# A hybrid encoder step on one core: a PSUM bank each for attention and memory, bias rows for two heads at a time, gates copied by ScalarE, the sample's keys fetched two steps sooner, and the rows of w_out in the order of their use

## The chip, the cores and the metric

The kernel runs on one core of a Trainium2 chip. The metric is the device time of one execution in microseconds (us). Three runs of the kernel before took 2756.32, 2762.39 and 2764.4 us; their median is 2762.39.

## The reference

One layer of an encoder computes one inference step for a prompt (2048 positions) and a sample group (8 requests of 16 positions), model width 1024, all in fp32.

```
h = RMSNorm(x) * g0
z = h @ w_in                  # q,k,v of 8 attention heads (64), q,k,v,o of 4 memory heads (128), 8 gates
A = attention: a chunk of 64 sees itself and 8 chunks before it, with a learned bias clipped at +-256
    (sample: 512 cached keys and its own 16)
B = matrix memory: decayed sum of k v^T with exp input gate, log-sigmoid forget gate, running maximum;
    h = num / max(|den|, exp(-m)), then RMSNorm by head, times g and sigmoid(o)
x = x + RMSNorm(concat(RMSNorm(A), B) @ w_out) * g1
x = x + RMSNorm(ConvFFN(RMSNorm(x) * g2)) * g3      # up-projection, causal conv of 3, GELU gate, down
```

Outputs are x of both groups, the last keys and values, the memory state and the conv halo.

## The kernel before

The program is written in a layer that allocates tiles from pools and lets a scheduler order the instructions. The scheduler takes them by their place in the source and moves them where its own model of time says that an engine would be free; each engine then runs its list strictly in order and waits on semaphores. So an edit of a few lines moves instructions on every engine.

The work of the first phase is a projection and, between its matmuls, two pipes of small units. The projection runs over 28 groups: two halves of the tiles (tile = 128 positions; tiles 0 to 7 and the sample, then 8 to 15) times 14 column groups of w_in (`va`, `qk` for attention, `qb`, `vo` for memory). Every product is three matmuls (L105, L106, L107): high times high, high times low, low times high part of fp32 numbers. A group accumulates in one of two PSUM banks `mm`. ScalarE empties it into a staging tile `st` (two of them, L237, L239) and stores that from its own DMA queue (L252, L288), and a 264-column group also holds the gates, which VectorE copied at L286.

The first pipe is attention (`att_stream`). `load_head` (L340 on) fetches a head's bias `nb`, queries and keys by SP's queue and splits them into high and low parts on ScalarE and VectorE. `att_unit` makes scores `s` in a two-bank PSUM tile `big`, adds the bias and takes the row minimum on VectorE, the exponent on ScalarE, transposes (`pt`), splits (`pth`, `ptl`) and multiplies by the values into `ot`; after two heads `ao` transposes the result, which goes to DRAM (`mixd`). The eight heads' bias comes from `relrow`: for every head a row `ext` of 767 numbers is written 128 times to DRAM (L317, 393 KB, SP's queue), two corners of 64x64 are overwritten by a large number (L322, POOL's queue, out of SBUF), and the result is read back along its diagonals. All eight heads are made so at the start. The sample's attention (`attention_sample`) runs over eight batches in two parts: keys (`sk`), scores `ss`, weights, values (`sv`, tail `svt`), result `sot`; keys and values use two buffers each of the tags `kh` and `kl`.

The second pipe is the memory (`mem_stream`): `prep_prompt` and `prep_sample` make cumulated gates, and `mlstm` runs over chunks of 128 positions for four heads. A chunk has two steps. The first computes scores and transposed keys in a PSUM tile `ms` (L701 on), the exponent `w` and the scaled keys `kw`; the second computes three products in a PSUM tile `ma` (L715 to L717) and updates the state `cst`. In the kernel before, a new chunk's first step may be issued ahead of the old one's second.

PSUM has eight banks: two for `mm`, two double ones for `big`, and two under the tag `sm`, which attention's `ot`, `ao`, `sot`, the memory's tiles and later the FFN's transposes take in turn.

`pump` steps the two pipes in turn so that the work of VectorE keeps a share of that of TensorE. At the last group `w_out_steps` casts the rows of w_out into high and low parts `wo` (L946 on), 128 rows at a time, two column halves each. Then `project` multiplies the 17 tiles by w_out, 48 matmuls a tile (24 for each half of the columns), with the transposes `mT_pt` of the next tile between the halves; in tiles 0 to 7 and the sample, `mT_pt` uses the two banks `mm`. Beside it, `folds` turns w_down into sums that the FFN uses, by DMAs of POOL's queue and subtractions on VectorE. When tile 8 is loaded, the two pipes are emptied (`drain`), the first phase's memory is released (`open_ffn`), and units that normalise and transpose finished tiles for the FFN (`h2_units`, `h2T_pt`, rows `x2r`) take the pipes' place. The FFN follows and fills the second half of the time; the change does not touch it, apart from where its transposes find their banks.

Of the kernel before, what the change touches and what calls it, by code (L numbers as in the profile page):

```python
# [50 lines left out]
def hymba_step(ctx: ExitStack, tc: tile.TileContext, I: dict, O: dict):  # L51
# [14 lines left out]

    def ps_sm(name):
        return psum.tile([P, 512], F32, tag="sm", name=name)
# [72 lines left out]
    pm = p1.enter_context(tc.tile_pool(name="pm", bufs=2))  # L141

# [128 lines left out]
    def group_rows(wh, wl, half, chunks, dst, name, width=256, out=None):  # L271
        for ci, tiles in enumerate(HALVES[half]):
            for j, t in enumerate(tiles):
                ch = chunks[ci]
                acc = ps_mm(f"{name}_{t}")
                for k in range(KT):
                    w = slice(k * width, (k + 1) * width)
                    tt = slice(j * P, (j + 1) * P)
                    mm3(acc[:, :width], ch[:, 0, k, tt], ch[:, 1, k, tt], wh[:, w], wl[:, w],
                        start=(k == 0), stop=(k == KT - 1))  # L280
                    if k % 4 == 3:
                        yield 1.3, 0.0
                stage = pa.tile([P, 384], F32, tag="st", name=f"{name}_st{t}", bufs=2)
                evac_scaled(stage[:, :256], acc[:, :256], None)
                if width > 256:
                    nc.vector.tensor_copy(gates[:, gate_ix(t), :], acc[:, 256:width])  # L286
# [6 lines left out]
    relrow = dt_([HA, P, SQ], "relrow")  # L293
# [9 lines left out]

    def build_bias():
        ext = dt_([HA, SQ], "ext")

        def unit():
# [8 lines left out]
            for h in range(HA):  # L316
                tc.keep_in_program_order(nc.sync.dma_start(relrow[h], ext[h:h + 1, :].broadcast_to([P, SQ])))  # L317
                yield 0.0, 0.0
                for r, c in ((0, 576), (64, 0)):
                    at = bias_src(h, P, 640)  # L320
                    at = bass.AP(at.tensor, at.offset + r * (SQ - 1) + c, [[SQ - 1, 64], [1, 64]])
                    nc.gpsimd.dma_start(at, big[r:r + 64])  # L322
                if h % 2:
                    yield 0.0, 0.0
# [56 lines left out]
    def att_unit(s, g2, j):  # L381
# [45 lines left out]
        ot = ps_sm(f"ot{h}_{i0}")  # L427
# [21 lines left out]
        ao = ps_sm(f"ao{pair}_{kg}")  # L449
# [94 lines left out]
    def cum_rows(ig, lf, nlf, r, trim, name):  # L544
        ba = ps_sm(f"ba{name}")
# [9 lines left out]
    def pack_columns(pk, name):  # L555
        pt = ps_sm(f"pkT{name}")
# [7 lines left out]
    def prep_prompt(half):  # L564
# [8 lines left out]
        rt = ps_sm(f"rt{half}")  # L573
# [9 lines left out]
        mp = ps_sm(f"mp{half}")  # L583
# [90 lines left out]
    def mlstm(h, half):  # L674
# [22 lines left out]
        def chunk(s, c):  # L697
# [4 lines left out]
            sp = ps_sm(f"ms{s.nm}_{c}")  # L702
# [12 lines left out]
            nc.tensor.matmul(acc[:, e:2 * e], q_, cst[h], start=True, stop=True)  # L715
            nc.tensor.matmul(acc[:, 0:e], w, s.va[:, c, :], start=True, stop=True)
            nc.tensor.matmul(acc[:, 2 * e:3 * e], kw, s.va[:, c, :], start=True, stop=True)  # L717
            nc.vector.scalar_tensor_tensor(cst[h], cst[h], dec[:, cc, h:h + 1], acc[:, 2 * e:3 * e],
                                           op0=ALU.mult, op1=ALU.add)
            nc.scalar.activation(num[:, c, :], acc[:, e:2 * e], AF.Identity, scale=col(1))  # L720
            nc.vector.tensor_tensor(num[:, c, :], num[:, c, :], acc[:, 0:e], op=ALU.add)
# [15 lines left out]
        for s in pairs:  # L737
            if s.pc < 3:
                yield load(pairs[s.pc + 1])
            yield chunk(s, 0)  # L740
            yield chunk(s, 1)

    def mlstm_sample(h):
# [6 lines left out]
        def own():  # L750
# [16 lines left out]
            sp = ps_sm(f"ms{nm}")  # L767
# [8 lines left out]
            acc = ps_sm(f"ma{nm}")  # L776
# [5 lines left out]
        def batches(bp):  # L782
# [13 lines left out]
            cu = ps_sm(f"cu{nm}_{bp}")  # L796
# [39 lines left out]
    def attention_sample(b0, b1):  # L836
# [18 lines left out]
        def scores(b):  # L855
            ks = halves(f"sk{b}")
# [3 lines left out]
            if b % 4 == 0 or b == b0:  # L860
                nc.sync.dma_start(own, kTs[:, :, b // 4 * 64:b // 4 * 64 + 64])
            yield 0.0, 0.0
# [34 lines left out]
        def values(b):  # L897
# [6 lines left out]
            yield 0.0, 0.0  # L904
            yield 0.0, 0.0
            yield 0.0, 0.0
            yield 0.0, 0.0
            ot = ps_sm(f"sot{b}")
# [28 lines left out]
    def w_out_steps():  # L937
# [5 lines left out]
        for k in range(KT):  # L943
# [9 lines left out]
            h_, l_ = big[-1][:, k % 3 * 2, :], big[-1][:, k % 3 * 2 + 1, :]  # L953
            for c in (slice(0, 512), slice(512, D)):
# [4 lines left out]
                else:  # L959
                    nc.scalar.copy(h_[:, c], raw[:, c])  # L960
                    nc.vector.tensor_tensor(l_[:, c], raw[:, c], h_[:, c], op=ALU.subtract)
                if k < 6:
                    yield 0.0, 0.6
            wo.append((h_, l_))
# [88 lines left out]
    def open_ffn():  # L1053

        p1.close()
        ffn.p3 = ctx.enter_context(tc.tile_pool(name="p3", bufs=2, reuse_waits="tile"))
# [939 lines left out]
```

## Time and profile before

| | |
|---|---|
| runs | 2756.32, 2762.39, 2764.4 us, median 2762.39 |
| profiled execution | 2761.56 us, span 2759.8 us |
| busy | PE 2659.9 us (96%), VectorE 1862.4 (67%), ScalarE 1417.6 (51%), POOL 700.7 (25%) |
| mean granted clock of TensorE | 0.988 |
| stages, from the page and the timeline | projection with attention and memory to about 1010 us, w_out to about 1330, FFN from there |

A line of a stretch gives the time, for each engine its busy time and in brackets its number of instructions, the granted clock, the share of DMA time and GB/s. A line of waits gives the waiting instruction, who released it, the total, the count and the longest. In a line of the timeline the first two numbers are start and duration, and square brackets hold the idle time of the engine before it and what ended that. PE is TensorE, DVE is VectorE, ACT is ScalarE.

### The profile page before, as it was taken

What the parts mean: (1) busy time and instruction counts of PE and PEld (TensorE: products, weight loads), DVE (VectorE), ACT (ScalarE), POOL (GpSimd) and SP (SyncE); (2) the same over time, 40 slices, a digit from 0 to 9 for tenths busy, and PEclk for the clock granted to TensorE, in tenths of its full rate; (3) what the DMA queues carried; (4) which work ended last, traced back from release to release, by engine and by line L of the source; (5) the groups of instructions that cost most, each with busy time, mean ns of one, the idle gap of its engine ahead of it and who ended that gap; (6) DMA issues with size and microseconds to landing.
All of it is one profiled execution on the core that took longest, in us unless ns stands there. A gap on an engine that the chain in (4) does not pass through costs nothing.

```text
span 2759.8 us, 47655 instructions
## 1 busy us (share of the span) xinstructions
PE 2659.9 (96%) x16459; PEld 2481.2 (90%) x16459; DVE 1862.4 (67%) x3536; ACT 1417.6 (51%) x2887; POOL 700.7 (25%) x1325
## 2 busy tenths in 40 slices
PE   8899999999999999979899999999999999999998
PEld 7899999999799998867799998889999878999976
DVE  5345445644355666556898998758888776899956
ACT  4345544533355665433454456655454665555554
POOL 1100000211000002344655542023333212466401
PEclk9999999999999999989999999999999999999999
DMA  5634454556743554469877768766786777788775
GB/s 173 171 114 138 122 186 140 172 176 196 225 135 116 157 178 146 146 228 308 298 246 215 214 198 265 251 208 195 223 219 192 228 252 238 213 246 237 253 257 183
DMA packets 333711, 555.70 MB, mean 201 GB/s; under 512 B 61762, under 2 KB 169374, under 8 KB 333150
## 3 DMA queue, kind: packets, MB, share of 16 engines
q1 hardware_dynamic: 250798, 405.03, 47.5%
q0 software_dynamic: 44080, 113.81, 14.1%
q10 hardware_dynamic: 38592, 33.83, 3.7%
q8 instruction: 129, 2.11, 0.3%
q14 instruction: 112, 0.92, 0.1%
HBM read 389.77 MB, written 172.18 MB: 204 GB/s over the span
## 4 chain that ended last, share of the span: by engine, by line
PE 41%; DMA 5%; DVE 4%; issue 2%; ACT 1%; POOL 0%; DVEq 0%; SPq 0%; POOLq 0%; ACTq 0%
PE uec L105 5%; PE uec L106 5%; PE uec L107 5%; PE dn L107 3%; PE dn L105 3%; PE dn L106 3%; PE ua L107 3%; PE ua L106 3%; PE ua L105 3%; DMA wu<-in_w_up 2%; PE dnm L107 1%; PE dnm L106 1%; PE dnm L105 1%; PE ub L107 1%; PE ub L106 1%
## 5 line engine op out<-in xcount | busy, mean ns | idle before, releaser
L105 PE MATMUL uec<-B,wuh 128*128 128x384 f32 (+1 forms) x720 | 236.6, 329 | 9.2 <-DVE ug L1495 5.9
L106 PE MATMUL uec<-B,wuh 128*128 128x384 f32 (+1 forms) x720 | 235.4, 327 | 0.0
L107 PE MATMUL uec<-B,wul 128*128 128x384 f32 (+1 forms) x720 | 234.3, 327 | 0.0
L1324 ACT CAST wuh<-wu 128x512 fp32r<-128x512 f32 x255 | 141.6, 618 | 102.6 <-PE uec L106 98.7
L107 PE MATMUL dn<-wdh,al 128*128 128x512 f32 x462 | 186.0, 403 | 3.4 <-DVE al L1325 3.4
L105 PE MATMUL dn<-wdh,ah 128*128 128x512 f32 x462 | 183.6, 397 | 5.9 <-ACT ah L1324 4.0
L1325 DVE TENSOR_TENSOR al<-ar,ah 128x768 fp32r<-128x768 f32 (+2 forms) x141 | 108.4, 779 | 118.4 <-ACT ah L1324 114.8
L106 PE MATMUL dn<-wdl,ah 128*128 128x512 f32 x462 | 182.8, 396 | 0.0
L1324 ACT CAST ah<-ar 128x768 fp32r<-128x768 f32 (+2 forms) x141 | 96.2, 692 | 153.2 <-PE dnm L106 113.9
L1325 DVE TENSOR_TENSOR wul<-wu,wuh 128x512 fp32r<-128x512 f32 x255 | 164.3, 682 | 2.4 <-ACT wuh L1324 2.4
L663 POOL TENSOR_SCALAR ad<-ad 128x2 f32<-128x2 f32 x32 | 6.3, 195 | 615.3 <-DVE ad L661 615.3
L410 DVE CUSTOM_DVE_ANT_0 tmp<-s,nb 128x640 f32<-128x640 f32 (+4 forms) x128 | 94.1, 737 | 100.1 <-PE s L400 99.5
L105 PE MATMUL vo<-wi_h,hT 128*128 128x256 f32 x544 | 155.5, 286 | 0.0
L107 PE MATMUL vo<-wi_h,hT 128*128 128x256 f32 x544 | 155.3, 285 | 0.0
L106 PE MATMUL vo<-wi_l,hT 128*128 128x256 f32 x544 | 154.9, 285 | 0.0
L1325 DVE TENSOR_TENSOR wdl<-wdr,wdh 128x512 fp32r<-128x512 f32 x231 | 145.3, 684 | 8.2 <-ACT wdh L1324 8.0
L105 PEld LDWEIGHTS uec<-B,wuh 128*128 128x128 f32 x720 | 135.2, 188 | 13.6 <-issue 6.8
L105 PE MATMUL qk<-hT,wi_h 128*128 128x384 f32 (+1 forms) x384 | 130.3, 339 | 9.9 <-ACT qk_st L239 6.2
L411 ACT ACTIVATE tmp<-tmp,mn 128x640 f32<-128x640 f32 (+4 forms) x128 | 97.7, 763 | 77.0 <-DVE mn L410 72.6
L106 PEld LDWEIGHTS uec<-B,wuh 128*128 128x128 f32 x720 | 135.4, 188 | 0.2
L107 PEld LDWEIGHTS uec<-B,wul 128*128 128x128 f32 x720 | 135.1, 188 | 0.0
L1324 ACT CAST wdh<-wdr 128x512 fp32r<-128x512 f32 x231 | 127.4, 619 | 11.8 <-PE uec L106 7.4
(473 smaller groups left out, 9101.8 us busy)
## 6 DMA issues: line engine op xcount, KB each, us to landing
wu<-in_w_up SPq DMA_DIRECT2D x220, 256.0 KB, 4.8
wu<-wsd SPq DMA_DIRECT2D x176, 256.0 KB, 4.7
wdr<-wtd SPq DMA_DIRECT2D x132, 256.0 KB, 5.1
wi_raw<-in_w_in SPq DMA_DIRECT2D x52, 512.0 KB, 4.2
wdr<-in_w_down SPq DMA_DIRECT2D x99, 256.0 KB, 4.7
wsd<-ws POOLq DMA_DIRECT2D x88, 256.0 KB, 4.8
ar<-ad_S SPq DMA_DIRECT2D x50, 384.0 KB, 4.0
kraw<-kTd SPq DMA_DIRECT2D x112, 128.0 KB, 3.1
```

Source lines behind the costliest of these rows:

```text
L105: nc.tensor.matmul(out, ah, bh, start=start, stop=False, skip_group_check=onto)
L106: nc.tensor.matmul(out, ah, bl, start=False, stop=False, skip_group_check=onto)
L107: nc.tensor.matmul(out, al, bh, start=False, stop=stop, skip_group_check=onto)
L410: nc.vector.tensor_tensor_reduce(o_, s_, b_, 1.0, 3e38, ALU.add, ALU.min, accum_out=mn)
L411: nc.scalar.activation(tmp[:, :n], tmp[:, :n], AF.Exp, bias=mn, scale=-1.0, accum_out=rsum[:, i % 4, hh:hh + 1])
L663: nc.gpsimd.tensor_scalar(ad, ad, 1.0 / DH, 0.0, op0=ALU.mult, op1=ALU.add)
L1324: nc.scalar.copy(h, r)
L1325: nc.vector.tensor_tensor(l, r, h, op=ALU.subtract)
```

## The change

Five edits. (1) In the first phase attention's `ot`, `ao` and `sot` use one PSUM bank of their own (`at`) and the memory's tiles another (`me`); the two banks `sm` exist only from the FFN on. A memory chunk now uses one tile: its three products overwrite scores and keys in the same bank, and the stream has an empty step (`bubble`) after each chunk, or the next load. (2) Bias rows of heads 0 and 1 are made at the start; those of head h + 2 when head h's second group of keys is loaded. The corners come from a copy in DRAM. (3) The gates are copied by ScalarE. (4) The sample's keys of the next batch are fetched in the second step of the values of this one. (5) For rows 6 and 7 of w_out the first column half of both is cast before the second.

The diff, cut to its core:

```diff
+    def ps_at(name):
+        return sm.pool.tile([P, 512], F32, tag="at", name=name, bufs=1)
+
+    def ps_me(name):
+        return sm.pool.tile([P, 512], F32, tag="me", name=name, bufs=1)
+
     def ps_sm(name):
-        return psum.tile([P, 512], F32, tag="sm", name=name)
+        return sm.pool.tile([P, 512], F32, tag="sm", name=name, bufs=2)
...
-                    nc.vector.tensor_copy(gates[:, gate_ix(t), :], acc[:, 256:width])
+                    nc.scalar.copy(gates[:, gate_ix(t), :], acc[:, 256:width])
...
+    def bias_rows(h):
+        tc.keep_in_program_order(nc.sync.dma_start(relrow[h], ext[h:h + 1, :].broadcast_to([P, SQ])))
+        for r, c in ((0, 576), (64, 0)):
+            at = bias_src(h, P, 640)
+            at = bass.AP(at.tensor, at.offset + r * (SQ - 1) + c, [[SQ - 1, 64], [1, 64]])
+            nc.gpsimd.dma_start(at, corner[r:r + 64])
...
-            for h in range(HA):
...
+            nc.sync.dma_start(corner, big)
+            for h in range(2):
+                bias_rows(h)
...
     def load_head(s):
         pair, kg, hh, h, nm = s.pair, s.kg, s.hh, s.h, s.nm
+        if kg == 1 and h < HA - 2:
+            bias_rows(h + 2)
...
-            sp = ps_sm(f"ms{s.nm}_{c}")
+            sp = ps_me(f"ms{s.nm}_{c}")
...
-            acc = ps_sm(f"ma{s.nm}_{c}")
-            nc.tensor.matmul(acc[:, e:2 * e], q_, cst[h], start=True, stop=True)
...
+            own, upd, old = sp[:, 0:e], sp[:, e:2 * e], sp[:, 2 * e:3 * e]
+            nc.tensor.matmul(old, q_, cst[h], start=True, stop=True)
...
         for s in pairs:
-            if s.pc < 3:
-                yield load(pairs[s.pc + 1])
             yield chunk(s, 0)
+            yield load(pairs[s.pc + 1]) if s.pc < 3 else bubble()
             yield chunk(s, 1)
+            yield bubble()
...
             nc.sync.dma_start(tail, vs[b * DS:(b + 1) * DS, :])
             yield 0.0, 0.0
+            if b + 1 < b1:
+                fetch(b + 1)
...
             for c in (slice(0, 512), slice(512, D)):
                 if k < 6:
+                    cast(k, raw, c)
                     yield 0.0, 0.6
+                elif k == 7:
+                    cast(6, late[:, :D], c)
+                    cast(7, late[:, D:], c)
```

What the scheduler makes of it, at three places. First POOL at the start, where it computes the scales of the first tiles (`n_4_ms`, `n_4_rs`: tile 4's mean square and its inverse root). Before:

```order
L94 TENSOR_TENSOR n_3_rs<-n_3_ms,nhalf 128x1
L88 TENSOR_SCALAR n_4_ms<-ssq_501 128x1
L94 TENSOR_TENSOR n_4_rs<-n_4_ms,nhalf 128x1
L88 TENSOR_SCALAR n_5_ms<-ssq_552 128x1
L94 TENSOR_TENSOR n_5_rs<-n_5_ms,nhalf 128x1
```

And now, with the corners of heads 0 and 1 (`relrow_301`, `relrow_302`):

```order
L100 TENSOR_TENSOR n_3_rs<-n_3_ms,nhalf 128x1
L318 DMA relrow_301<-corner 64x64
L94 TENSOR_SCALAR n_4_ms<-ssq_513 128x1
L318 DMA relrow_301<-corner 64x64
L318 DMA relrow_302<-corner 64x64 x2
L100 TENSOR_TENSOR n_4_rs<-n_4_ms,nhalf 128x1
```

The four corner writes, which stood behind the scales of all tiles, have moved between the two instructions of tile 4's.

Second SP's queue from the first bias rows to the first keys of the second group, in the new order (`nb` is a head's bias, `xr` a tile's x, `wi_raw` weights, `relrow_303` and `relrow_304` the rows of heads 2 and 3):

```order
L314 DMA relrow_301<-ext 128x767
L314 DMA relrow_302<-ext 128x767
L1256 DMA wi_raw_404<-in_w_in 128x1024
L232 DMA xr_562<-in_x_prompt 128x1024
L1256 DMA wi_raw_509<-in_w_in 128x1024
L356 DMA nb_0_1165<-relrow_301 128x640
L356 DMA nb_0_1229<-relrow_302 128x640
L232 DMA xr_663<-in_x_prompt 128x1024
...
L314 DMA relrow_303<-ext 128x767
L363 DMA qraw_1_1389<-qTd_1_98 64x512 x2
L366 DMA kraw_1_0_1390<-kTd_0_81 64x512 x2
```

The bias of the first two heads is read ahead of tile 7's x (`xr_663`); before, the bias rows stood behind all loads of x (the first four between two loads of weights, `wi_raw_945` and `wi_raw_1161`), and the reads of the bias behind them.

Third TensorE in the projection by w_out, around a memory chunk (`ms`, `ma`) and the transposes of the next tile (`mT_pt`). Before:

```order
L77 MATMUL mT_pt_14352<-ident,mr_14269 128x128 x4
L715 MATMUL ma_10_1_13118<-cst_313,mqk_10_12793 128x129
L716 MATMUL ma_10_1_13118<-mvo_10_12795,w_10_1_13074 128x129
L717 MATMUL ma_10_1_13118<-mvo_10_12795,kw_10_1_13076 128x129
L77 MATMUL pt_12_13152<-ident,tmp_12_13092 128x128 x5
L399 MATMUL s_14_13238<-kh_3_12827,qs_3_12829 128x320
L400 MATMUL s_14_13238<-kl_3_12828,qs_3_12829 128x320
```

And now, at one of the closest handovers of the memory's bank:

```order
L727 MATMUL ms_14_1_13495<-cst_325,mqk_14_13380 128x129
L728 MATMUL ms_14_1_13495<-mvo_14_13382,w_14_1_13498 128x129
L729 MATMUL ms_14_1_13495<-mvo_14_13382,kw_14_1_13500 128x129
L83 MATMUL mT_pt_14007<-ident,mr_13835 128x128 x4
L83 MATMUL mT_pt_14014<-ident,mr_13835 128x128 x4
L715 MATMUL ms_8_0_13716<-mqk_8_13672 128x128
L83 MATMUL ms_8_0_13716<-ident,mqk_8_13672 128x128
L111 MATMUL wo_1_14032<-wo_13346,mt_13758 128x512
```

Before, attention's matmuls (`pt`, `s`) still stood between those of the projection here; now they have all gone before, and only memory chunks are left. In the new order attention's last matmul stands behind 120 of the projection's 816 (before: 353), the memory's last behind 431 (before: 517), and 92 stand between the memory's last and the FFN's first transposes `h2T_pt` (before: 59).

More of the change, by code (lines that the diff above doesn't have):

```diff
@@ L290, in group_rows @@
                     nc.scalar.dma_start(out[s - 3][:, 0 if s == 4 else t % 4, :], stage[:, :256])
-    relrow = dt_([HA, P, SQ], "relrow")
+    relrow = [dt_([P, SQ], f"relrow{h}") for h in range(HA)]
+    ext = dt_([HA, SQ], "ext")
+    corner = dt_([P, 64], "corner")
     def raw_tile(name):
@@ L713, in chunk @@
             num = s.num
-            acc = ps_sm(f"ma{s.nm}_{c}")
[L715 to L721, printed above, removed]
+            own, upd, old = sp[:, 0:e], sp[:, e:2 * e], sp[:, 2 * e:3 * e]
+            nc.tensor.matmul(old, q_, cst[h], start=True, stop=True)
+            nc.tensor.matmul(own, w, s.va[:, c, :], start=True, stop=True)
+            nc.tensor.matmul(upd, kw, s.va[:, c, :], start=True, stop=True)
+            nc.vector.scalar_tensor_tensor(cst[h], cst[h], dec[:, cc, h:h + 1], upd, op0=ALU.mult, op1=ALU.add)
+            nc.scalar.activation(num[:, c, :], old, AF.Identity, scale=col(1))
+            nc.vector.tensor_tensor(num[:, c, :], num[:, c, :], own, op=ALU.add)
             yield 0.65, 0.47
@@ L853, in halves, with fetch @@
             return [pa.tile([P, 1024], F32, tag=tag, name=f"{name}{tag}", bufs=2) for tag in ("kh", "kl")]
-        def scores(b):
-            ks = halves(f"sk{b}")
+        keys = {}
+        def fetch(b):
+            keys[b] = ks = halves(f"sk{b}")
             for i in range(2):
@@ L861, in scores @@
                 nc.sync.dma_start(own, kTs[:, :, b // 4 * 64:b // 4 * 64 + 64])
+        def scores(b):
+            if b not in keys:
+                fetch(b)
+            ks = keys.pop(b)
             yield 0.0, 0.0
@@ L907, in values @@
             yield 0.0, 0.0
[L908 removed]
+            ot = ps_at(f"sot{b}")
             for kk in range(5):
```

38 lines of the change are left out of this document (17 added, 21 removed).

## The prediction

> **What bounds the kernel now.** I read the page first, then the stretches, then the waits of PE, then the stretches around those waits.
>
> ```profile
> span 2759.8 us, 47655 instructions
> PE 2659.9 (96%) x16459; PEld 2481.2 (90%) x16459; DVE 1862.4 (67%) x3536; ACT 1417.6 (51%) x2887; POOL 700.7 (25%) x1325
> ```
>
> TensorE is busy 2659.9 of 2759.8 us, and the change keeps every matmul: it can win only from what TensorE loses, 99.9 us of idle time and the slow time behind it. Next, stretches (columns: us, busy of PE, PEld, DVE, ACT, POOL with instructions, granted clock, DMA share, GB/s): the start, the tail of attention and memory under the w_out matmuls, and the way into the FFN.
>
> ```profile
> core 0: us, PE busy (x) PEld busy (x) DVE busy (x) ACT busy (x) POOL busy (x), PEclk, DMA share, GB/s
> 12.00:45.00 33.00, 32.46 (x248) 31.98 (x248) 22.49 (x30) 19.51 (x34) 6.23 (x14) 1.00 0.53 168
> 1000.00:1180.00 180.00, 173.02 (x1030) 150.73 (x1028) 114.17 (x262) 99.56 (x260) 41.94 (x87) 0.98 0.54 168
> 1180.00:1330.00 150.00, 125.83 (x559) 99.91 (x558) 87.81 (x142) 51.61 (x116) 71.73 (x134) 0.91 0.81 272
> ```
>
> The last row loses 24.2 us and a clock of 0.91; nothing in it is saturated (DVE 59%, DMA 0.81), so these are chains of latency. PE's waits, those that the argument uses (us in total, times, longest):
>
> ```profile
> PE h2T_pt L1111 <- DVE x2r L1103: 7.7, 3, 6.0
> PE qk L105 <- ACT qk_st L239: 6.2, 1, 6.2
> PE ss L874 <- DMA sk6kh<-in_cache_k: 3.2, 1, 3.2
> PE qk L105 <- ACT qk_st L237: 3.1, 1, 3.1
> PE va L105 <- DVE gates L286: 2.3, 1, 2.3
> PE mT_pt L77 <- DVE mr L995: 2.3, 2, 2.1
> PE ms L703 <- DVE w L709: 1.9, 1, 1.9
> PE wo L106 <- DVE wo L961: 1.4, 1, 1.4
> PE ma L715 <- DVE attT L442: 1.1, 1, 1.1
> ```
>
> A wait costs more than its length. Stretches around them, PE alone, with two of dense work (57 to 64 only 384-column matmuls, 1206 to 1216 only w_out):
>
> ```profile
> 57.00:64.00 7.00, 7.00 (x42) 1.00 0.77 226
> 77.00:90.20 13.20, 8.91 (x36) 0.74 0.75 146
> 104.40:114.00 9.60, 3.41 (x11) 0.64 0.96 284
> 150.00:400.00 250.00, 250.00 (x1835) 1.00 0.46 140
> 534.00:541.00 7.00, 4.68 (x26) 0.76 0.56 174
> 709.00:718.20 9.20, 5.92 (x30) 0.81 0.90 320
> 1012.00:1036.00 24.00, 19.78 (x121) 0.86 0.76 229
> 1140.00:1200.00 60.00, 54.45 (x283) 0.97 0.59 188
> 1206.00:1216.00 10.00, 10.00 (x45) 1.00 0.79 248
> 1217.00:1241.00 24.00, 14.00 (x51) 0.64 0.77 267
> ```
>
> A projection matmul issues every 7.00/42 = 0.167 us, one of w_out every 10/45 = 0.222. So 77 to 90.2 needed 36 x 0.167 = 6.0 us and took 13.2 (7.2 lost), 104.4 to 114 lost 9.6 - 11 x 0.167 = 7.8, and 1217 to 1241 at least 24 - 51 x 0.222 = 12.7.
>
> **The bias rows.** Both early waits (9.3 us, 15.0 lost) lie beside the eight writes of bias rows and their sixteen corners.
>
> ```profile
> L317 SPq DMA_DIRECT2D relrow<-ext x8: 469/576/2191, 58.8 to 101.6; - x8
> ...
> DMA to landing us min/median/max: 7.1/8.2/9.5
> ...
> 109.57 0.62 ACT L363 CAST kh<-kraw 128x512 fp32r<-128x512 f32 x1 [4.29 <-DMA kraw<-kTd]
> 110.10 0.48 ACT L239 ACTIVATE qk_st<-qk 128x384 f32<-128x384 f32 x1
> ```
>
> ScalarE waited 4.29 us in its order for keys (issued behind the last two row writes) and only then emptied the bank that TensorE wanted. With two heads first and six spread over the next pairs, queues are shorter. But after the change the rows of heads 2 and 3 still stand before key loads on SP's queue. A full win is 15.0, none 0; I take 9.0, the middle and a little, since one write at a time replaces two to six. Spreading adds six writes of 7.1 to 9.5 us beside stores that double-buffered stages wait for; between 150 and 400 us PE was never idle, so they have cover: 1.0 (0 to 4).
>
> **What they cost at the start.** The first two heads' corners now stand in POOL's queue between the scales of tiles 3 and 4, and the loads of their bias stand in SP's queue ahead of tile 7's x. In the trace:
>
> ```profile
> L322 POOL DMA_DIRECT2D relrow<-outside x16: 532/532/759, 66.2 to 110.4; - x16
> ...
> DMA to landing us min/median/max: 2.8/7.0/8.1
> ...
> 12.55 0.29 SPq L312 DMA_DIRECT2D ext<-relf  x1
> 19.99 0.19 POOL L88 TENSOR_SCALAR n_ms<-ssq 128x1 f32<-128x1 f32 x1 [5.09 <-ACT hT L229]
> 25.20 0.65 SPq L225 DMA_DIRECT2D xr<-in_x_prompt  x1
> 37.84 0.33 SPq L225 DMA_DIRECT2D xr<-in_x_sample  x1
> ```
>
> A row write can go out at about 16 us (behind ext's landing), lands 7 us later, and so POOL gets to tile 4's scale near 24 to 26 instead of 20. In the new order 47 more matmuls of tiles 2 and 3 (0.13 us each by 33/248) stand ahead of tile 4's transposes, 6 us: that covers it. Tile 7's x waits for a corner's landing (7.0 in the median), so it goes out at 30 to 32 instead of 25.2; the sample's x, whose place tile 7 frees, follows at 40 or later instead of 37.84. Cost 3.0 (0 to 8).
>
> **Gates by ScalarE.**
>
> ```profile
> L286 DVE COPY gates<-va x17: 153/157/167, 23.2 to 560.0; 128x8 f32<-128x8 f32 x17
> ```
>
> Seventeen copies of 0.157 us leave DVE; in its order they stood behind splits and held a bank. 534 to 541 needed 26 x 0.13 = 3.4 us and took 7.0: 3.6 gone. ScalarE, which has just emptied the same bank, is 51% busy; with no cover, and at twice the time each, the copies would cost 17 x 0.314 = 5.3, and I take nothing.
>
> **The clock.** The stretch at 534 shows a granted clock of 0.76 after a wait of 2.3 us. The Trainium skill, "TensorE: Matmul & The Clock Gate", What's actually happening, says that the clock halves after an idle window of about 3.4 us and comes back after as long a busy one. This trace halves it after shorter waits; by the page the gates would bring 2.3, not 3.6.
>
> **Keys two steps sooner.** 3.2 us of wait, and half a clock for 3.4 us behind it (0.81 over 9.2 us is 1.7): 4.9. The load is moved behind the values' loads of the batch before, whose waits for buffers it now shares on SP. In the new order the eight batches stand evenly, with 72 projection matmuls or so from one to the next (12 us at 0.167 for 2 MB, 175 GB/s, below the 320 of the stretch at 709). I take 4.5 (0 to 5).
>
> **A bank each.** The wait of ma for attT (1.1) goes. But memory now reuses one bank for scores, update and next scores, 98 tiles in all, and attention one for 88. Between two of them TensorE mostly has other work: of 184 handovers 5 have under 2 us, counting what stands between them in the order at the trace's rates. Five times that 1.1 us would be 5.5; I take 1.5 (0 to 5.5).
>
> **Rows of w_out.** The first half of tile 0 no longer waits for the second half's columns: 1.4 and its clock. 1012 to 1036 lost 4.2 of idle and 24 x 0.14 = 3.4 of clock over three waits; I take 3.0 (1.4 to 7.6).
>
> **The moved tail.** The extra steps of memory and the free bank move work: attention now ends 120 w_out matmuls into the projection instead of 353, memory at 431 instead of 517 of 816. That is both cost and gain. Cost: (353 - 120)/48 = 4.9 tiles more without attention between them. 1140 to 1200, where attention had ended, is idle for 5.55 us and 1.8 of clock in 60 us, 4.5 tiles; so 4.9 tiles would cost 8.0, and the memory chunks that remain there cover some: 6.0 (0 to 28). Gain: the FFN's first transposes need the space of the phase that ends.
>
> ```profile
> 1204.05 0.35 DVE L718 SCALAR_TENSOR_TENSOR cst<-cst,dec,ma 128x129 f32<-128x129 f32 x1 [1.67 <-PE ma L717]
> 1209.34 0.13 DVE L1058 MEMSET halo<- 128x88 f32 x1
> 1223.05 1.28 DVE L1103 SCALAR_TENSOR_TENSOR x2r<-x2r,n_rs,g 128x1024 f32<-128x1024 f32 x1 [0.74 <-POOL n_rs L94]
> ```
>
> From the last chunk to the scaled row passed 20.3 us. TensorE had 59 w_out matmuls for it (13.1 us) and waited 6.0 at the half clock that follows. Now 92 stand there (20.4 us): the wait goes, with most of the 12.7 lost. I take 9.0 (4 to 12.7).
>
> **Sum.** -9.0 + 1.0 + 3.0 - 3.6 - 4.5 - 1.1 + 1.5 - 3.0 + 6.0 - 9.0 = -18.7 us. The profiled execution took 2761.6 (1.8 outside its span), 0.8 under the median of 2762.4; 2761.6 - 18.7 = 2743. With the page's clock rule for the gates the sum would be -17.4.
>
> **Rivals.** First, the rows don't really move: with the writes still beside the keys, both early waits stay and the start is paid in full (8.0): -18.7 + 9.0 + 5.0 = -4.7, 2757. For it: ScalarE's order still has the cast of the keys ahead of a bank to empty. Against: less is in flight, and the store of the first wait (L237) has no row write left before it. Second, idle time only moves into the projection: if the 4.9 uncovered tiles pay what the tile at 1180 to 1189 pays, its waits for mr (2.1) and for w (1.9) and the clock behind them (1.8 by the row of that stretch), 5.8 each, they cost 28 instead of 6: +3, 2765. For it: the banks of mT_pt are those of w_out there. Third, slower: the single banks. A matmul into the one bank must wait until ScalarE and VectorE have read it. If one handover in four waits 1.1 us, 46 x 1.1 = 51 instead of 1.5: 2792; it decides from (18.7 + 8.3)/1.1 = 25 waits on. The Trainium skill, "Perfetto Trace Analysis", Matmuls, has independent groups rotate through different banks so that emptying one overlaps the next; by that rule this rival is due. Against it: the trace holds one such wait (1.1, of ma for attT), and the new order keeps the handovers apart.
>
> **Chances.** The forecast 0.62 (on its own 2725 to 2757: two or three terms at their bounds, not all), the first rival 0.13, half of it a small gain, the second 0.16, slower 0.09. A difference under 0.3% (8.3 us) can't be told from none. Faster: 0.62 + 0.08 = 0.70; within 0.3%: 0.05 + 0.16 = 0.21; slower 0.09. The range leaves out the third rival and the ends of the others: 2722 to 2765.
>
> **What would show it.** Right: no wait of qk for qk_st over 2 us before 130 us; none of va for gates; none of ss for a key; the first h2T_pt under 2 us; clock 0.95 or more from 1180 to 1330. PE's loss from 12 to 50 us up by some 3 us. Wrong: a row of waits of ms or ot for num, cst or attT (single banks), or of mT_pt for mx and mr that sum to over 20 us (moved idle time), or 15 us lost in the first 50 us.

## The result

Four runs of the changed kernel took 2728.1 to 2736.4 us, median 2731.5; the kernel before 2756.3 to 2764.4 (four runs, one more than above), median 2761.0. The ratio is 0.9899, with a 95% interval of 0.9878 to 0.9920: 28 us faster by the ratio (the medians lie 29.5 apart). A second series, of the same code built and loaded once more, took 2737.2 to 2744.2 (six runs), median 2741.1, beside 2758.6 for the kernel before (17 runs): 0.9934, interval 0.9918 to 0.9949, 18 us faster; it had been expected at 2728 to 2736. The two series don't overlap; what that means for the experiments stands at their head. The forecast was 2743, between 2722 and 2765, a gain of 18.7. One run of the experiment e3 below took 3696 us at a mean granted clock of 0.654 and is left out of e3's median.

A correction to what stands above: the counts of w_out matmuls behind which attention and memory end (353 and 120, 517 and 431) are each one tile, 48, too high. In the traces attention's last stands behind 305 of them before and 72 after, memory's last behind 469 and 383, and the FFN's first transposes behind 528 and 475. The differences, with which the forecast worked (59 and 92 matmuls of cover, 4.9 tiles), are the same.

### The profile page after: what moved, and what is told of

Read it like the earlier page. It is cut to its first block, busy times and chain, and to the rows that moved or that the text cites. A ratio compares the mean times of both kernels' runs of the same rounds, so it can differ in the third digit from the quotient of the medians.

```text
span 2734.6 us, 47676 instructions
## 1 busy us (share of the span) xinstructions
PE 2652.1 (97%) x16459; PEld 2476.5 (91%) x16459; DVE 1862.9 (68%) x3519; ACT 1418.7 (52%) x2904; POOL 685.8 (25%) x1325
## 4 chain that ended last, share of the span: by engine, by line
PE 45%; DVE 3%; DMA 3%; issue 1%; ACT 1%; POOL 0%; DVEq 0%; POOLq 0%; SPq 0%; ACTq 0%
PE uec L111 6%; PE uec L112 6%; PE uec L113 6%; PE dn L113 4%; PE dn L111 4%; PE dn L112 4%; PE ua L113 3%; PE ua L112 3%; PE ua L111 3%; PE dnm L113 2%; PE ub L113 1%; PE dnm L112 1%; PE ub L111 1%; PE ub L112 1%; PE dnm L111 1%
## 5 line engine op out<-in xcount | busy, mean ns | idle before, releaser
L435 DVE TENSOR_TENSOR ptl<-pt,pth 128x640 fp32r<-128x640 f32 (+4 forms) x128 | 93.6, 737 | 58.6 <-ACT pth L434 57.7
```

The source lines that it names most:

```text
L435: nc.vector.tensor_tensor(s.ptl[:, sl, qc], ptv, s.pth[:, sl, qc], op=ALU.subtract)
```

## The profile after

The head of the page of the changed kernel:

```profile
span 2734.6 us, 47676 instructions
...
PE 2652.1 (97%) x16459; PEld 2476.5 (91%) x16459; DVE 1862.9 (68%) x3519; ACT 1418.7 (52%) x2904; POOL 685.8 (25%) x1325
```

TensorE's idle time has gone from 99.9 to 82.5 us. For what the slower clock costs beside it, a stretch is read so: its width less busy time times granted clock is what TensorE lost there, idle and slow together. First the kernel before, stretch by stretch (us, PE, PEld, DVE, ACT, POOL, clock, DMA share, GB/s):

```profile
12.00:75.00 63.00, 59.59 (x413) 57.60 (x414) 36.09 (x89) 26.54 (x50) 10.78 (x23) 1.00 0.54 161
75.00:130.00 55.00, 44.52 (x254) 42.95 (x254) 14.87 (x38) 17.34 (x40) 5.41 (x12) 0.88 0.58 155
...
600.00:700.00 100.00, 99.09 (x786) 91.39 (x785) 43.67 (x153) 35.62 (x105) 14.04 (x49) 1.00 0.65 199
700.00:775.00 75.00, 67.56 (x587) 58.73 (x586) 27.38 (x59) 30.81 (x69) 1.26 (x4) 0.98 0.67 207
1000.00:1050.00 50.00, 45.70 (x297) 41.35 (x296) 35.40 (x79) 32.73 (x81) 8.94 (x19) 0.93 0.73 216
1050.00:1215.00 165.00, 158.37 (x879) 134.67 (x879) 97.23 (x230) 77.28 (x211) 44.80 (x91) 0.99 0.49 154
1215.00:1330.00 115.00, 94.78 (x412) 74.62 (x411) 69.36 (x95) 41.15 (x85) 59.94 (x111) 0.90 0.89 302
1330.00:1600.00 270.00, 258.78 (x1443) 252.27 (x1442) 250.16 (x386) 131.50 (x207) 150.21 (x213) 0.99 0.73 235
```

And the changed kernel:

```profile
12.00:75.00 63.00, 56.27 (x374) 53.88 (x375) 33.93 (x68) 26.68 (x57) 10.22 (x19) 0.95 0.46 150
75.00:130.00 55.00, 49.70 (x288) 47.30 (x286) 19.30 (x60) 20.40 (x52) 3.32 (x7) 0.94 0.60 150
...
600.00:700.00 100.00, 94.29 (x891) 83.36 (x890) 38.71 (x125) 36.71 (x104) 9.97 (x33) 1.00 0.81 249
700.00:775.00 75.00, 72.37 (x511) 70.73 (x510) 43.85 (x116) 38.08 (x90) 6.88 (x22) 1.00 0.45 134
1000.00:1050.00 50.00, 48.45 (x405) 48.05 (x404) 32.23 (x73) 32.92 (x76) 2.17 (x6) 1.00 0.50 153
1050.00:1215.00 165.00, 153.05 (x759) 123.83 (x758) 89.25 (x188) 62.45 (x171) 61.52 (x122) 0.97 0.63 201
1215.00:1330.00 115.00, 107.10 (x524) 88.51 (x523) 81.26 (x110) 48.49 (x96) 53.60 (x96) 1.00 0.90 317
1330.00:1600.00 270.00, 265.33 (x1504) 262.51 (x1503) 253.32 (x397) 134.98 (x216) 139.53 (x220) 0.99 0.71 220
```

From 1215 to 1330 us the kernel before lost 115 - 94.78 x 0.90 = 29.7 us, and the changed one 115 - 107.10 x 1.00 = 7.9. That is 21.8 of the 25.2 us by which the spans differ. The other stretches shown add up to 7 us less, out of terms of both signs: the start loses 9.5 instead of 3.4, the stretch with the two early waits 8.3 instead of 15.8, the sample's keys 2.6 instead of 8.8 while 600 to 700 just ahead of them loses 5.7 instead of 0.9, 1000 to 1050 loses 1.5 instead of 7.5, w_out with memory beside it 16.5 instead of 8.2, and the FFN's entrance 7.3 instead of 13.8. Of those not shown, 400 to 600 loses 1.6 instead of 6.3 and 775 to 1000 4.8 instead of 0.6. From 12 to 2700 us all this comes to 28 us, not 25.2: the clock is printed to two places, which leaves a loss open by up to half a us for every 100 us, and a fixed stretch doesn't hold quite the same work in both kernels.

PE's waits that answer to the forecast's list:

```profile
PE cus L809 <- DMA cs<-in_state_c: 3.1, 2, 2.2
PE va L111 <- ACT gates L293: 2.9, 2, 1.5
PE ms L727 <- DVE w L721: 2.8, 4, 1.4
...
PE ms L715 <- DVE num L732: 1.5, 2, 1.1
...
PE h2T_pt L1139 <- DVE x2r L1131: 0.5, 1, 0.5
```

No qk waits for qk_st, no ss for a key and no ma for attT; h2T_pt's 7.7 us are 0.5. The waits for gates have not gone, they only have another engine's name: 2.3 on VectorE before, at 536 us; now 1.4 at 28 us and 1.5 at 555 on ScalarE. New is the wait of the sample's memory for its state, cs (3.1, in the stretch from 600 to 700). The 2.8 for w are waits for the product's input, and of the waits of ms only the 1.5 for num are for the single bank.

## The experiments

Medians of twelve kernels, each timed in five rounds beside the kernel before, and what TensorE lost in the stretches above (worked out in the same way from the stretches of each one's trace). "Ends" gives the w_out matmuls behind which attention's last, memory's last and the FFN's first transposes stand.

| kernel | us | ratio (95%) | ends | 12-75 | 75-130 | 700-775 | 1000-1050 | 1050-1215 | 1215-1330 | 1330-1600 |
|---|---|---|---|---|---|---|---|---|---|---|
| before | 2755 to 2761 | 1 | 305, 469, 528 | 3.4 | 15.8 | 8.8 | 7.5 | 8.2 | 29.7 | 13.8 |
| changed | 2731.5 | 0.9899 (0.9878-0.9920) | 72, 383, 475 | 9.5 | 8.3 | 2.6 | 1.5 | 16.5 | 7.9 | 7.3 |
| e12 changed, again | 2741.1 | 0.9934 (0.9918-0.9949) | 72, 383, 475 | 9.9 | 7.6 | 1.7 | 1.9 | 19.2 | 8.5 | 9.5 |
| e1 bias rows only | 2745.4 | 0.9948 (0.9929-0.9966) | 208, 352, 480 | 8.8 | 5.0 | 4.4 | 6.5 | 18.1 | 10.4 | 8.5 |
| e2 edit 1 only | 2738.2 | 0.9929 (0.9915-0.9942) | 72, 383, 475 | 3.0 | 11.6 | 2.1 | 0.2 | 16.6 | 7.7 | 5.9 |
| e3 edits 3, 4, 5 only | 2755.4 | 0.9990 (0.9975-1.0006) | 305, 469, 528 | 3.9 | 16.6 | 8.3 | 8.0 | 7.4 | 28.7 | 10.2 |
| e4 empty steps only | 2739.6 | 0.9931 (0.9916-0.9945) | 120, 332, 471 | 2.8 | 15.0 | 10.7 | 1.2 | 22.5 | 7.1 | 4.4 |
| e5 banks, no steps | 2737.0 | 0.9927 (0.9904-0.9950) | 72, 336, 480 | 3.5 | 13.4 | 2.3 | 1.6 | 12.7 | 7.5 | 5.8 |
| e6 cover only | 2753.0 | 0.9987 (0.9972-1.0002) | 305, 469, 568 | 3.8 | 15.6 | 8.0 | 10.4 | 6.1 | 30.8 | 11.9 |
| e7 whole without banks | 2736.3 | 0.9935 (0.9912-0.9959) | 120, 332, 480 | 5.7 | 5.3 | 4.7 | 0.6 | 18.6 | 7.5 | 3.4 |
| e8 rows behind x | 2731.9 | 0.9909 (0.9886-0.9931) | 72, 383, 475 | 4.0 | 8.6 | 3.0 | 2.1 | 17.9 | 8.5 | 9.5 |
| e9 whole, less cover | 2750.3 | 0.9970 (0.9958-0.9981) | 72, 383, 432 | 9.9 | 8.5 | 0.8 | 2.1 | 25.8 | 4.0 | 13.8 |
| e10 whole without 3, 4, 5 | 2736.3 | 0.9914 (0.9898-0.9931) | 72, 383, 475 | 8.0 | 6.5 | 2.2 | 2.2 | 18.4 | 11.7 | 5.4 |
| e11 banks, rows, no steps | 2744.1 | 0.9944 (0.9928-0.9959) | 72, 336, 480 | 4.0 | 11.1 | 3.0 | 0.8 | 13.8 | 14.6 | 9.8 |

The medians of the kernel before lie between 2755.4 and 2761.0 in its four series. Those of the changed kernel lie 9.5 us apart, and its runs within a series spread by 7 to 8. Three chips were used, one for e1 to e4, one for e5 to e8 and one for e9 to e12; the record doesn't name that of the first series, so the 9.5 us may come from the chip as well as from the loading. So a kernel is read against the kernel before, and a difference of under some 10 us between two kernels counts here only where a wait or a stretch of the traces shows it as well.

### The bias rows alone (e1)

```diff
-            for h in range(HA):
...
+            for h in range(2):
+                bias_rows(h)
...
+        if kg == 1 and h < HA - 2:
+            bias_rows(h + 2)
```

> The kernel before with edit 2 alone (bias rows two heads at a time). In the new order attention ends after 208 w_out matmuls instead of 305, memory after 352 instead of 469, and 128 matmuls stand ahead of the FFN's first transposes instead of 59, although no line there is touched. Theory A (the forecast's: a term belongs to the place of its edit; the tail belongs to edit 1): only the start changes, by 75 to 130 us some 6.6 less lost and from 12 to 75 us some 6.2 more, as the trace of the whole change shows: 2758 to 2763. Theory B (the tail is a matter of the order that comes out, whichever edit brings it; 128 matmuls are 28 us of cover for a chain of 20): the first wait of h2T_pt for x2r is under 1 us, the stretch 1200 to 1350 loses some 16 us less, and the total is 2738 to 2748.

Measured 2745.4, 14 us faster by the ratio of 0.9948. Two of its stretches:

```profile
75.00:130.00 55.00, 51.54 (x319) 49.27 (x318) 19.75 (x55) 22.71 (x58) 3.29 (x7) 0.97 0.60 157
...
1215.00:1330.00 115.00, 107.81 (x508) 87.52 (x507) 79.81 (x108) 47.74 (x95) 60.61 (x108) 0.97 0.91 318
```

At its own place it gains what was forecast and pays for it: 75 to 130 loses 5.0 instead of 15.8, 12 to 75 loses 8.8 instead of 3.4. But 1215 to 1330 loses 10.4 instead of 29.7, though not a line of that stage is edited, and the first wait of h2T_pt is gone (four later ones for x2r sum to 3.7). Theory B holds, theory A falls. (The old unit for the bias took thirteen steps of attention's pipe, the new one three. That this is what moves attention up is argued from the code, not shown.)

### Edit 1 alone (e2), and its two halves (e4, e5)

Edit 1 is the separate banks, the chunk's products in the scores' bank, and the empty steps. e4 is only the latter:

```diff
         for s in pairs:
-            if s.pc < 3:
-                yield load(pairs[s.pc + 1])
             yield chunk(s, 0)
+            yield load(pairs[s.pc + 1]) if s.pc < 3 else bubble()
             yield chunk(s, 1)
+            yield bubble()
```

> The kernel before with edit 1 alone (a bank each, products of memory in one tile, empty steps). The order ends attention after 72 w_out matmuls, memory after 383, and has 92 ahead of the first FFN transposes, as the whole change has. Theory A (the tail belongs to edit 1): the first h2T_pt wait goes (16 us) and so do the waits of mt and ug between 1250 and 1600 us (13 together); -20 to -29 with the early waits of qk for qk_st and the gates' wait still there: 2732 to 2742. Rival (the tail's gain needs another edit as well, the banks cost): the h2T_pt wait stays over 2 us or waits of ms for num and cst sum to over 5 us: 2750 or more.

> The kernel before with only the empty steps of the memory's stream (and its loads one step later), banks as before. Attention ends after 120 w_out matmuls, memory after 332, 139 ahead of the first FFN transposes. If the tail is a matter of the order (theory B): h2T_pt's first wait is gone and the total is 2735 to 2748, the banks themselves being worth nothing or a little less than nothing. If the separate banks are what frees the tail (theory A): the h2T_pt wait or its like stays, 2755 or more.

> The kernel before with the separate banks alone: one bank for attention, one for memory, the products of a chunk in the scores' bank, and none of the empty steps, so a new chunk's scores may be issued right behind the old one's products. The order ends attention after 72 w_out matmuls, memory after 336, and has 144 ahead of the first FFN transposes. If the forecast's third rival holds (46 handovers at 1.1 us), the waits of ms, ot and pt for num, cst, attT and mx grow by some 50 us: 2775 or more. If only the order counts: the first h2T_pt wait is gone as with the empty steps alone, 2738 to 2746.

Measured: 2738.2, 2739.6 and 2737.0 (1 us under the range expected for e5), ratios 0.9929, 0.9931 and 0.9927. Either half gives what both give, and each alone about as much as the whole change in its second series. e4's tail:

```profile
1050.00:1215.00 165.00, 150.02 (x760) 123.38 (x759) 89.59 (x209) 64.42 (x183) 56.75 (x116) 0.95 0.60 194
1215.00:1330.00 115.00, 107.86 (x523) 87.80 (x522) 80.33 (x107) 50.36 (x97) 62.48 (x104) 1.00 0.92 316
```

And in e5, with single banks and no empty step between the chunks, the only waits of ms for the bank's reader (num is added out of it), with its tail:

```profile
PE ms L710 <- DVE num L727: 1.6, 3, 0.6
```

```profile
1215.00:1330.00 115.00, 107.54 (x528) 89.52 (x527) 81.25 (x111) 46.98 (x91) 54.65 (x97) 1.00 0.91 315
```

1.6 us in three waits, where the third rival wanted 51: single banks cost next to nothing here, even without the steps that keep the chunks apart. (The same wait is 3.2 in e2 and 3.3 in e11; with shared banks it is 1.5 in e1 and 1.4 in e7.) And what the changed kernel gains in the tail isn't the banks' own either, since the empty steps, with the banks as before, gain it too.

### The three local edits alone (e3), and the whole without them (e10)

```diff
-                    nc.vector.tensor_copy(gates[:, gate_ix(t), :], acc[:, 256:width])
+                    nc.scalar.copy(gates[:, gate_ix(t), :], acc[:, 256:width])
...
+            if b + 1 < b1:
+                fetch(b + 1)
...
+                elif k == 7:
+                    cast(6, late[:, :D], c)
+                    cast(7, late[:, D:], c)
```

> The kernel before with edits 3, 4 and 5 (gates by ScalarE, keys sooner, w_out rows in order of use). The order of attention and memory under w_out is that of before (305, 469, 528). Theory A (the terms are local): no wait of va for gates on VectorE (-4), none of ss for a key (-5), none of wo for the second half's columns (-1.4 to -3), the first h2T_pt wait still 6 us: 2748 to 2753. Rival (what is gained early is waited for again at a chain that doesn't move, the FFN's first row or a DMA): within 4 us of before.

> The changed kernel without edits 3, 4 and 5 (gates on VectorE, the sample's keys as before, w_out rows as before); banks, bias rows and empty steps stay, and the order of attention and memory is that of the changed kernel. If the three are worth nothing here either, as they were alone: within 4 us of the changed kernel. If they need the new order to pay (the forecast's 11 us): 2738 or more.

Alone they change nothing that can be told (0.9990, interval 0.9975 to 1.0006), and the whole without them (2736.3) was not slower than the whole beside it (2741.1). It lies 4.8 us from either series of the changed kernel, just over the 4 expected. The rival's number holds in e3, but not its reason: nothing was gained early and waited for later. The waits simply stayed, as e3's list shows:

```profile
PE h2T_pt L1127 <- DVE x2r L1119: 6.4, 2, 4.9
...
PE ss L881 <- DMA sk6kh<-in_cache_k: 2.4, 1, 2.4
...
PE va L105 <- ACT gates L286: 1.9, 1, 1.9
...
PE wo L106 <- DVE wo L972: 1.4, 1, 1.4
```

Why they stayed can be read in the trace of before, one step behind the name that the wait was given. The gates, on ScalarE and on VectorE:

```profile
534.48 1.06 ACT L229 ACTIVATE hT<-xr 128x1024 fp32r<-128x1024 f32 x1 [0.81 <-DMA xr<-in_x_prompt]
...
535.78 0.36 ACT L237 COPY va_st<-va 128x256 f32<-128x256 f32 x1
```

```profile
536.17 0.17 DVE L286 COPY gates<-va 128x8 f32<-128x8 f32 x1
```

ScalarE itself left the bank only at 535.78 + 0.36 = 536.14, because it had waited for x and squared it first; VectorE's copy ended at 536.34. Taking VectorE out could save 0.2 us, not 2.3. The rows of w_out, on VectorE:

```profile
1029.56 0.23 DVE L509 TENSOR_SCALAR hgm<-hgm 128x128 f32<-128x128 f32 x1 [1.73 <-DMA hgm<-in_g_mlstm]
1029.71 1.28 DVE L961 TENSOR_TENSOR wo<-wor,wo 128x512 fp32r<-128x512 f32 x2
```

The cast that TensorE waited for stood behind a 1.73 us wait for the memory's gain, which no order of w_out rows removes. And the keys, on SP's queue, in the trace of before and in e3:

```profile
705.17 0.42 SPq L901 DMA_DIRECT2D sv5kl<-in_cache_v  x1
705.63 0.43 SPq L858 DMA_DIRECT2D sk6kh<-in_cache_k  x1
```

```profile
706.15 0.42 SPq L908 DMA_DIRECT2D sv5kl<-in_cache_v  x1
706.62 0.43 SPq L860 DMA_DIRECT2D sk6kh<-in_cache_k  x1
```

Two steps sooner in the source, and the load goes out right behind the same load of values as before. In the changed kernel the wait is gone, but not by edit 4: in e10, without it, no ss waits for a key either, and 700 to 775 loses 2.2. The likely reason is that the batches stand farther apart there: the scores of batches 4 to 7 follow each other after 15 to 19 us, before after 13 to 15.

### More cover, and less (e6, e9)

```diff
-        pipes[:] = [Pipe(h2_units(0, lead=6)), Pipe(iter([]))]
+        pipes[:] = [Pipe(h2_units(0, lead=16)), Pipe(iter([]))]
```

That is e6, on the kernel before; e9 is the changed kernel with lead=0.

> The kernel before with one number changed: the FFN's first unit starts after 16 empty steps instead of 6. Attention and memory stay where they were (305 and 469 w_out matmuls), but 99 w_out matmuls (22 us) stand ahead of the first h2T_pt instead of 59 (13 us). If cover is what the tail gains from (theory B's mechanism): the 6.0 us wait for x2r and its half clock go, 1215 to 1250 loses 10 to 16 us less, and the later waits of mt and ug fall with them or stay: 2742 to 2750. Rival (the transposes merely come later and the FFN's first matmuls wait for them instead, or the backlog of VectorE and POOL is what has to be gone): 2754 or more.

> The changed kernel with the FFN's first unit started after no empty step instead of 6. Attention and memory stay (72 and 383 w_out matmuls), but only 49 w_out matmuls (10.9 us) stand ahead of the first h2T_pt instead of 92 (20.4 us). If cover decides whether that transposition waits: a wait for x2r of 9 us with the slower clock behind it, 1180 to 1250 loses 9 to 14 us more, and as the units then come earlier the FFN's entrance (1250 to 1600) gets back some of it: 2733 to 2743. Rival (it is enough that memory ends early): no wait over 2 us, within 4 us of the changed kernel.

e6 measured 2753.0 (0.9987, no difference that can be told). The first wait for x2r is gone, and w_out ends at 1306.3 us instead of 1327.1. Then TensorE stands still for 15.7 us at the FFN's first matmul:

```profile
PE ua L105 <- ACT wuh L1324: 16.2, 2, 15.7
```

```profile
1306.73 0.58 ACT L1128 COPY b<-h2T_pt 128x512 f32<-128x512 f32 x1 [2.06 <-PE h2T_pt L1111]
...
1308.09 0.70 SPq L1119 DMA_DIRECT2D lated<-t  x1
1309.13 7.06 SPq L1336 DMA_DIRECT2D wu<-in_w_up  x4
```

The later transposes issue later stores (lated), and the FFN's weights (wu) stand behind these on SP's queue; the store just before the one shown writes out a `b` that had waited for its transposition until 1306.7 us (first row). So the rival's mechanism holds, though 2753.0 is 1 us under its number: cover alone shifts the wait to the next stage. e9 shows the other side: 2750.3, beside 2741.1 for the changed kernel in the same series. With 49 matmuls of cover the wait for x2r is back, at 1203 us. It is 4.9 us long and not the 9 expected, since the 49 matmuls with what stands between them took 18 us instead of 10.9:

```profile
PE h2T_pt L1139 <- DVE x2r L1131: 6.4, 4, 4.9
```

The stretch with that wait, 1050 to 1215, loses 25.8 in e9 and 19.2 in e12. The total missed the 2733 to 2743 expected: the FFN's entrance gave little back (4.0 instead of 8.5 from 1215 to 1330, but 13.8 instead of 9.5 from 1330 to 1600). Both things are needed: cover for the chain behind memory's last chunk, and transposes that are early enough to be out of the way of the FFN's weights. An earlier end of memory gives both. The kernels whose memory ends behind 332 to 383 matmuls lose 4 to 15 us from 1215 to 1330, the three with 469 lose 28.7 to 30.8.

### The banks taken out, and the start mended (e7, e8, e11)

e7 is the changed kernel with the two shared banks of before (edit 1's empty steps stay). e8 loads the source of the bias rows late:

```diff
-        rel.append(raw_tile("reln")[:HA, :SQ - 383])
+        rel.append(rows_tile("pth", [P, D], "reln")[:HA, :SQ - 383])
...
-    load_bias()
...
+                load_bias()
                 heads.append(build_bias)
```

e11 is e8 without the empty steps.

> The changed kernel with attention and memory back in two shared banks: bias rows, gates, keys, w_out rows and the empty steps stay. Attention ends after 120 w_out matmuls, memory after 332, 148 ahead of the first FFN transposes. If the separate banks are worth nothing themselves: within 5 us of the changed kernel, 2728 to 2738. If they free the bank that attention's output waited for: 2742 or more, with waits of ma and ot for attT and w.

> The changed kernel with the first two heads' bias rows behind the loads of all tiles' x (their source is loaded into a buffer that the sample's x frees), so that POOL's scales of tiles 4 to 7 and SP's load of tile 7's x have no corner ahead of them. If the start lost 6.2 us to these queues: 12 to 75 us loses 3.5 us instead of 9.7 and the total is 2724 to 2728. Rival (the rows are then late for the first scores): the loss moves to 75 to 130 us, 2731 or more.

> The changed kernel without the empty steps and with the first bias rows behind the loads of x: what the runs so far leave as the best of each edit. Order: attention 72, memory 336, 144 w_out matmuls ahead of the first FFN transposes. From the traces: 6 less at the start than the changed kernel, 3 to 5 less between 1050 and 1600: 2718 to 2726. Rival (the start's loss only moves behind 75 us, and the tail is at its floor): 2727 to 2734, the same as the changed kernel.

e7 measured 2736.3, between the changed kernel's two series: the separate banks aren't needed for the gain. e8 measured 2731.9 (0.9909). The start is mended just as expected, since tile 4's scale (the first of the two rows) has no corner ahead of it any more and the corners follow all scales:

```profile
19.79 0.19 POOL L94 TENSOR_SCALAR n_ms<-ssq 128x1 f32<-128x1 f32 x1 [4.86 <-ACT hT L236]
...
57.07 2.25 POOL L318 DMA_DIRECT2D relrow<-corner  x4 [13.02 <-DMA relrow<-ext]
```

```profile
12.00:75.00 63.00, 58.98 (x410) 56.94 (x411) 36.49 (x82) 28.18 (x61) 8.47 (x18) 1.00 0.50 161
```

It loses 4.0 there instead of 9.5, and the loss has not moved to 75 to 130 us (8.6, where the changed kernel has 8.3). But the total missed its 2724 to 2728, and whether the whole is 5.5 faster for it can't be told beside two series of the same code that differ by 9.5. e11, at 2744.1, missed its 2718 to 2726 and also the rival's 2727 to 2734: its tail (14.6 from 1215 to 1330) was worse than that of e5, which has the same order there. No version was found that is shown to beat the changed kernel.

## Why the prediction was right, and where it wasn't

The time, its sign and the mechanism at both ends of the kernel came out. The number came out partly because terms that were too large and a term that was too small cancelled.

**The start, right and undersized.** The forecast had POOL get to tile 4's scale near 24 to 26 us, tile 7's x go out at 30 to 32 and the sample's at 40 or later. POOL's queue and SP's in the changed kernel:

```profile
23.09 0.73 POOL L318 DMA_DIRECT2D relrow<-corner  x1 [7.99 <-DMA relrow<-ext]
23.89 0.18 POOL L94 TENSOR_SCALAR n_ms<-ssq 128x1 f32<-128x1 f32 x1
24.13 1.54 POOL L318 DMA_DIRECT2D relrow<-corner  x3
```

```profile
27.93 0.82 SPq L356 DMA_DIRECT2D nb<-relrow  x2
...
31.94 0.33 SPq L232 DMA_DIRECT2D xr<-in_x_prompt  x1
...
41.90 0.33 SPq L232 DMA_DIRECT2D xr<-in_x_sample  x1
```

It cost 6.1 instead of 3.0 (within 0 to 8), though not where the forecast looked. The 47 matmuls did cover tile 4's late scale: its transposes waited for nothing. The idle time, 3.3 us more than before, came from other places: at 28 us TensorE waited 1.4 for ScalarE, which had itself waited 3.2 for weights; at 34 and 35 us 1.1 for split transposes; and the sample's transposes, behind its late x, waited 1.8 instead of 1.1. The other half is the clock, which was halved from 51 to 58 us, after that last wait and during one of 1.1. The kernel before waited 1.1 and 1.1 at the same place and kept a clock of 1.00.

**The early waits, right.** 9.0 forecast; 7.5 less lost from 75 to 130, 8.2 in the second trace, 10.8 in e1. Without edit 2 the waits of qk for qk_st stay (4.2 in e2, 5.0 in e5). The 1.0 for spreading the writes came out too: 130 to 400 loses 1.2 instead of 0.0.

**Gates, keys and w_out rows, wrong: 11.1 us credited.** The step that failed is the same in all three: "of a wait of X for Y, remove Y". X's length was taken as the gain. e3 measured none of it, for the reasons shown there: the engine or queue named was itself held by something that the edit doesn't touch. The changed kernel loses less at these places (4.7 less from 400 to 600, 6.2 from 700 to 775, 6.0 from 1000 to 1050), but so do kernels that have none of these edits (e10 loses 1.5, 2.2 and 2.2 there). Of the forecast's signs, the one that no va waits for gates is the one that failed.

**The banks, right.** 1.5 was forecast for the handovers, and the changed kernel's waits of ms for num are 1.5. That the two agree to the tenth is chance: the wait is 1.5 in e1 too, with shared banks, and lies between 0.5 and 3.3 in the kernels with single ones. The wait of ma for attT (1.1) is gone. The third rival would have made the kernel slower; e5 speaks against it directly. The Trainium skill's rule beside it, to rotate independent groups through different banks ("Perfetto Trace Analysis", Matmuls), is not borne out by the runs of this kernel, where such waits sum to 1.6 us in e5. That other work stands between two uses of a bank is the likely reason; no run tested it.

**The uncovered tiles, near in size, the reason not shown.** 6.0 forecast, 8.3 in the first trace and 11.0 in the second (1050 to 1215). But the term was counted by where attention ends, and the loss of that stretch doesn't follow it: 12.7 in e5 (behind 72 matmuls), 22.5 in e4 (120), 18.1 in e1 (208).

**The first transposes of the FFN, right in kind and mis-sized.** The term had 9.0, at most 12.7; the stretch 1215 to 1330 got back 21.8 (21.2 in the second trace) and 1330 to 1600 another 6.5 (4.3). The bound was taken from the 24 us around the first wait alone, and it was what they lost at least: by their clock they lost 24 - 14.00 x 0.64 = 15.0. More waits stood behind them, the longest 4.2 us for mt at 1314 us. VectorE was late with that mt because it had waited for the FFN's weights:

```profile
1311.35 0.69 DVE L1341 TENSOR_TENSOR ws<-wu,wu 128x512 f32<-128x512 f32 x1 [3.49 <-DMA wu<-in_w_up]
...
1313.29 1.22 DVE L212 TENSOR_TENSOR mt<-mT_pt,mt 128x1024 fp32r<-128x1024 f32 x1
```

SP's queue issued these weights behind and between stores of late transposes, as in e6: from 1299 us on, in the changed kernel from 1286 on. That the other waits, up to those of the FFN's gates near 1500 us, hang on the same chain is argued, not shown. The cover itself (92 matmuls enough, 49 not) is shown by e9. But the forecast's comparison, 20.4 us of matmuls for a chain of 20.3, held in part by luck, since both sides were off: in the changed kernel 28.4 us passed from memory's last matmul to the end of the scaled row, and the 92 matmuls with what stands between them took 31.0.

**Chances.** The second rival (idle time only moves into the projection) did move 8 to 11 us there, a third of what it asked for. The first (the rows don't move) fell.

**Open.** Why the planner lets memory end earlier when single steps are added to its pipe, or taken from attention's, was not followed up. Nor was the cause of the 9.5 us between the two series of the same code. In their traces the loss, idle time and slower clock taken together, is spread over many places, and TensorE's busy time is 2652.1 in one and 2655.4 in the other.

## What to carry to other kernels

Before a wait is counted as a gain, follow its releaser one step further back: what was that engine or queue itself waiting for? The three edits that failed that test gained nothing that could be told. In a program whose order comes out of pipes and a scheduler, compare the order far from the edit first: a few empty steps at one place (e4) were worth as much as the whole change in its second series, through a stage that they don't touch. And a chain that is late at a stage's entrance can cost several times its first wait (here 21.8 us or more for 6.0), so bound it by the whole stretch until TensorE is dense again.

## What the runs showed of the hardware

A wait's length doesn't say whether the clock falls. In the changed kernel's trace TensorE waited 2.19 us at 631 us for cs and 2.07 us at 772 us for qb_st (columns: us, PE busy, clock, DMA share, GB/s):

```profile
628.00:640.00 12.00, 9.81 (x110) 1.00 0.87 247
770.00:782.00 12.00, 9.93 (x72) 0.86 0.79 244
```

The longer one left the clock at 1.00, the shorter halved it for some 3.4 us (0.86 over 12). The Trainium skill, "TensorE: Matmul & The Clock Gate", What's actually happening, has the clock judged by free-running windows of about 3.4 us. Where a wait falls in such a window would explain the difference, and the halvings in these traces do come in steps of that length: 3.4 us here, and in the kernel before 3.4 at 537 us, 6.8 at 83 and at 107, and 17.1 at 1223, at the 6.0 us wait. But the page speaks of an idle window, and both waits here are shorter than one. At these two places a wait of about 2 us cost its own length and between nothing and 12 x 0.14 = 1.7 us more.
